# A hybrid decoder layer on one core: gate chunks one head group later, memory K/V beside the last heads, inputs and weights prepared earlier

## The chip, the cores and the metric

The kernel runs on one core of a Trainium2 chip. The metric is the device time of one execution in microseconds (us). A profiled execution gives a trace of every instruction on the core's engines: TensorE (PE, its weight loads apart as PEld), VectorE (DVE), ScalarE (ACT), GpSimd (POOL) and SyncE (SP, which issues DMAs here). "L437" means line 437 of the kernel.

## What is computed

One layer of a decoder for 512 tokens of width 2048, all in float32:

```python
xn = rmsnorm(h, g_mix)
q_a, ..., c_q, c_kv, k_r, gate_a, gate_b = split(xn @ w_in)   # one combined projection
o_a = nsa_attention(...)          # 16 heads: compressed blocks, and window/selected keys
o_b = mla_attention(c_q, c_kv, k_r, ...)                      # 16 heads, low-rank q and k/v
h += (sigmoid(gate_a) * (o_a @ w_o_nsa) + sigmoid(gate_b) * (o_b @ w_o_mla)) @ w_out
h += memory_cross_attention(rmsnorm(h), rmsnorm(mem))         # 4 heads, 256 memory tokens
h += square(relu(rmsnorm(h) @ w_ff1)) @ w_ff2
return rmsnorm(h, g_final)
```

## The kernel before

**Precision.** Each float32 operand is split into a high and a low part (`split`: ACT casts a copy, L444, DVE subtracts, L445), and each product is three matmuls of the parts (`mm`, L437 to L439; in the later stages L1725 to L1727). So TensorE needs ACT and DVE to prepare everything that it reads.

**Chunks.** Up to the attention's end, the kernel goes through `chunk`s: four PSUM banks of 128 tokens by up to 512 columns, 16 steps of k (4 in `mla_q`, 2 in `mla_kv`), 12 matmuls a step. Weights come through one stream `W` (three raw units, three split ones; the loads are on SP's queue, L272). `gate(c)` is one such chunk: columns of the first gate, tanh on ACT (L1151), written to DRAM (`d_g`).

**Side work.** The attention heads are generators in a queue (`Side`). After each group of matmuls a chunk calls `side.run(rate / 4)`, and each whole step that has come together queues a few instructions of a head: scores, softmax, transposes, values. A head item is 11 steps, a group of four heads 44. A group whose heads aren't ready spends its steps for nothing. Beside this runs `side.post`, the work behind a chunk: for `mla_q` four ropes on POOL (L521 to L524), then four transposes of heads (L537); for `mla_kv` the four transposes. At a chunk's last k, `end_post` queues all that is left of it.

**Order of `mla`.** `gate(0)`, `mla_q(0)`, `gate(1)`, `mla_kv(0)`. Then for three groups: the heads of the group before become side work, `mla_q(q + 1)`, a gate chunk (`gate(2)`, `gate(3)`; in the third group `mem_k` instead), `mla_kv(q + 1)`. `mem_load` brings the memory rows (loads L1279 and L1283; split L447/L448, squares on ACT and POOL); it is started between `gate(3)` and `mla_kv(2)`, and takes steps at the k of `mla_kv(2)` and `mla_q(3)`. `mem_v` stands last. The rates are in `T`: `rf` for the first group, `rm` for the others, `rk`, `rv` for the memory chunks, `rg` for the gates.

**`mix` and its three stages.** `Gates` (the second gate), `Mixed` (the two output projections, gated) and `Out` (`w_out`) multiply with seven block products in place of eight: 14 passes each, a pass of four units, a unit a 128 by 1024 block of weights and 12 matmuls. A unit's block may be a sum of two or three blocks of weights: the first is loaded by SP (L1513), the others are added by an accumulating load from POOL's queue (L1520) into the same buffer, after the sum before has been split. `prep(i)` casts the units up to i + 1 (`high`, L1525 on ACT), splits those up to i (`low`, L1530 on DVE) and asks for loads up to i + 2 + `LOADS`; it is called with the current unit + `AHEAD`, which is 3. `stat` and `stat_low` (L1607, L1612) prepare the activations of the next pass. `use` takes a pass's banks.

`Gates.x_in` loads a block of the input (L1929, on SP) and multiplies it by the gains, eight products on POOL (L1932). `mix` loads two of the four blocks, calls `loads(4)`, ends the stream, loads the other two, and then prepares the first units (`ahead`), with two side steps behind each. In the first seven passes of `Gates.run` the rest of the heads is side work at rate `rg`.

In `Mixed.use`, when a block is complete, DVE multiplies it by the gate (L2055, 128 by 1024) and, for the second projection, adds it to the first (L2060), at once for both halves.

Buffers come from 40 slots of 128 by 1024, handed out in the order in which they came free, and five pairs, whose areas are lent once the attention is done (`attended`).

Of the kernel before, what the change touches and what calls it, by code (L numbers as in the profile page):

```python
# [28 lines left out]
AHEAD, LOADS = 3, 3  # L29
ZEROS = 9  # L30
T = dict(pace=0.75, r0=4.0, r1=4.4, rm=2.6, rf=2.5, rk=0.8, rv=1.8, rg=1.4, rs=2)
# [365 lines left out]
class Layer:  # L397
# [747 lines left out]
    def gate(self, c, rate):  # L1145

        nc = self.nc

        def evac(tt, ps):
            g = self.Rv(tt, 512)  # L1150
            nc.scalar.activation(g, ps, AF.Tanh, scale=self.rxh[:, tt:tt + 1])  # L1151
            nc.scalar.dma_start(self.d_g[0, tt, :, 512 * c:512 * c + 512], g)

        self.chunk("ga", c, 512, evac, rate)
# [56 lines left out]
    def mla(self, rate):  # L1211

        self.gate(0, T["rf"])
        qs = self.mla_q(0, T["rf"])
        self.gate(1, T["rf"])
        ks, vs = self.mla_kv(0, T["rf"])
        ml = iter(())

        def load(n):
            return lambda k: [next(ml, None) for _ in range(n)]  # L1220

        for q in range(3):
            self.side.add(self.mla_attend(q, qs, ks, vs))
            qs = self.mla_q(q + 1, rate, load(2))
            if q < 2:
                self.gate(2 + q, rate)
            if q == 1:
                self.put(*self.X)
                ml = self.mem_load()
            if q == 2:  # L1230
                drain(ml)
                self.mem_k(T["rk"])
            ks, vs = self.mla_kv(q + 1, rate, load(4))
        self.side.add(self.mla_attend(3, qs, ks, vs))
        self.side.add(self.flush())
        self.mem_v(T["rv"])


    def mix(self):

        self.put(*self.R)
        g, m = Gates(self), Mixed(self)
        self.lp = []
        self.put(*self.cpairs)
        self.lend_pairs([self.pairs.get() for _ in self.cpairs])
        for a in ((0, 0), (1, 0)):
            g.x_in(*a)
        g.loads(4)
        self.side.end_post()
        self.W.end()  # L1250
        for a in ((1, 1), (0, 1)):
            g.x_in(*a)
        for i in range(4):
            g.ahead(i)
            for _ in range(T["rs"]):
                self.side.step()
        g.run(T["rg"], m)
        return m.run()
# [13 lines left out]
    def mem_load(self):  # L1272
        nc = self.nc
        self.MX = []
        self.mslots = [self.slots.get() for _ in range(8)]
        st, sl = self.halves(6)
        self.macc, self.macc_slot = st[4][:, :256], sl[2]
        for j in range(3):
            nc.sync.dma_start(st[j], self.a["memT"][j])  # L1279
        for j in range(8):  # L1280
            b = st[j % 4]
            if j + 3 < 8:
                nc.sync.dma_start(st[(j + 3) % 4], self.a["memT"][j + 3])  # L1283
            for e in range(2):
                k = 2 * j + e
                x, s = b[:, e * 256:e * 256 + 256], self.mslots[j][:, 512 * e:512 * e + 512]
                h = HL(s[:, :256], s[:, 256:])
                self.split(h, x, self.gains[:, G_MEM + k:G_MEM + k + 1])
                self.MX.append(h)
                self.sumsq(x, k, st[5][:, e * 256:e * 256 + 256], self.macc)  # L1290
                yield
        self.put(*sl[:2])

    def mem_k(self, rate):
# [15 lines left out]
        for h in range(4):  # L1310
            ps = self.ft("mk", h, self.MX, rate, n=256, on_k=on1 if h == 1 else None)
            if h:
                evac(h - 1, last)
            last = ps
        evac(3, last)

    def mem_v(self, rate):
# [3 lines left out]
        for u in range(8):  # L1321
            w = self.W.get(("mv", u, 0))
# [129 lines left out]
class Mlp:  # L1452
# [17 lines left out]
    TAG, TAG1 = "f2", "f1"  # L1470
    LAST = (5, 0, 1, 2, 3, 4, 6)
# [165 lines left out]
    def run(self, out):  # L1637
# [9 lines left out]
        for p in range(last):  # L1647
# [10 lines left out]
            for j in range(4):  # L1658
                i = 4 * p + j
                self.copies()  # L1660
                self.prep(i + AHEAD)
# [248 lines left out]
class Gates(Mlp):  # L1910
# [3 lines left out]
    TAG1 = "gs"  # L1914

# [42 lines left out]
    def run(self, rate, m):  # L1958
# [3 lines left out]
        for p in range(last + 1):  # L1962
            n = p % 7
            if p == 1:
                k.lend_pairs([k.pairs.get()])
# [9 lines left out]
            for j in range(4):  # L1975
                if k.late is None and k.prev is None and len(k.lp) < N_PAIRS:
                    k.attended()
                if p < last or j < 2:
                    self.prep(4 * p + j + AHEAD)
# [11 lines left out]
class Mixed(Mlp):  # L1991
# [3 lines left out]
    TAG = "wo"  # L1995

    def __init__(self, k):
        self.begin(k)
        self.A, self.R, self.g = {}, {}, {}

# [26 lines left out]
    def use(self, p, ps):  # L2027
# [22 lines left out]
        for t in range(2):  # L2050
            r = c, 2 * a + t, b
            g = self.g.pop(r[1:])
            if n < 6:
                x = R.pop(r) if c else R[r]
                v.scalar_tensor_tensor(g if c else x, g, 1.0, x, op0=OP.add, op1=OP.mult)  # L2055
                if c:
                    k.put(x)
            if c:
                x = R[0, 2 * a + t, b]
                v.tensor_add(x, x, g)  # L2060
            k.put(g)
# [14 lines left out]
    def run(self):  # L2076
# [4 lines left out]
        for p in range(last + 1):  # L2081
# [10 lines left out]
            for j in range(4):  # L2092
                if p < last or j < 2:
                    self.prep(4 * p + j + AHEAD)
# [4 lines left out]
                if p == last:  # L2099
                    out.ahead(j)  # L2100
                self.part(p, j, ps, range(2))
# [8 lines left out]
class Out(Mlp):  # L2110
# [7 lines left out]
    TAG = "w2"  # L2118
    COPIED = ((), (), (8, 9, 10), (11, 12, 13))
# [58 lines left out]
    def run(self):  # L2178
# [4 lines left out]
        for p in range(last + 1):  # L2183
# [9 lines left out]
            for j in range(4):  # L2193
                self.prep(4 * p + j + AHEAD)
                if j == 0:
                    self.blocks(p + 1)
                if p < last and j < 2:
                    (self.stat_low if j else self.stat)(p + 1, 0)
                if p < 3 and j % 2:
# [85 lines left out]
```

## Time and profile before

| | us |
|---|---|
| median of 3 runs (2881.62 to 2883.32) | 2883.11 |
| the profiled execution, whole | 2878.02 |
| its span, first to last instruction | 2876.2 |
| end of `gate(1)` (last tanh L1151) | 669 |
| end of `gate(2)` | 747 |
| end of `gate(3)` | 826 |
| evacuation of `mla_kv(3)` (L1189) | 898 to 901 |
| evacuation of `mem_v` (L1331), start of `mix` | 937 |
| first block matmul of `Gates` (L1725) | 950 |
| first evacuation of `Mixed` (L2039) | 1170 |

The times of the lower rows count from the span's start. A group's busy time is the sum over its instructions; a wait is the idle time of an engine in front of an instruction, with the instruction or the DMA that ended it. A window's row gives its length, then the busy time of each engine with the number of instructions, then the granted clock of TensorE (1.00 is full), the busy share of the DMA engines and GB/s. A row of the view in order of time gives start, duration, engine, line, operation, tiles, shape and count, and in brackets the wait before it.

### The profile page before, as it was taken

To read this page: it belongs to the slowest core of one execution; us is meant where nothing else is said; L and a number is where in the kernel's file an instruction comes from. 1 tells how busy PE (TensorE), PEld (TensorE's weight loads), DVE (VectorE), ACT (ScalarE), POOL (GpSimd) and SP (SyncE) were. 2 spreads that over 40 slices of the span, in tenths; PEclk is the share of its full clock that TensorE was granted. 3 is DMA by queue.
4 is the path that set the end of the run, shared out by engine and by line. 5 is a ranking of instruction groups with operands and counts; after the bars stand their busy time and mean duration, and the time that the engine had idled before them with its cause. 6 is when DMAs were issued, how large, how long until landed. Compare 5 with 4: busy or idle time off the path is not lost.

```text
span 2876.2 us, 37039 instructions
## 1 busy us (share of the span) xinstructions
PE 2785.0 (97%) x13428; PEld 2331.8 (81%) x13428; DVE 2036.1 (71%) x3215; ACT 1581.9 (55%) x2650; POOL 484.8 (17%) x708
## 2 busy tenths in 40 slices
PE   9999999999989599999999999999999999999998
PEld 8888889888869477777878888888888888888887
DVE  6446767654567576678776787776776788888888
ACT  5435556644556466543465676666666544444445
POOL 4130110011120511111100111111111111111111
PEclk9999999999999799999999999999999999999999
DMA  5231112222233678998742788888899998899986
GB/s 181 86 98 62 63 58 63 74 84 95 92 109 99 180 185 229 263 235 240 185 110 74 177 219 223 200 203 207 217 228 221 248 226 221 221 221 225 245 230 154
DMA packets 158888, 485.29 MB, mean 169 GB/s; under 512 B 16112, under 2 KB 40816, under 8 KB 158704
## 3 DMA queue, kind: packets, MB, share of 16 engines
q0 software_dynamic: 50688, 184.57, 34.1%
q1 hardware_dynamic: 83264, 268.20, 27.0%
q10 hardware_dynamic: 24752, 30.15, 3.0%
q8 instruction: 105, 1.72, 0.2%
q14 instruction: 79, 0.65, 0.1%
HBM read 447.21 MB, written 35.65 MB: 168 GB/s over the span
## 4 chain that ended last, share of the span: by engine, by line
PE 75%; issue 8%; DMA 6%; DVE 5%; ACT 3%; POOL 3%; ACTq 0%; POOLq 0%; SPq 0%; DVEq 0%
PE mm L1726 8%; PE mm L1727 8%; PE mm L437 8%; PE mm L1725 8%; PE mm L439 8%; PE mm L438 8%; PE st L1725 5%; PE st L1727 5%; PE st L1726 5%; DMA s<-wts 3%; DMA d<-wts 2%; PE st L674 2%; DVE s L1530 1%; PE st L438 1%; PE st L439 1%
## 5 line engine op out<-in xcount | busy, mean ns | idle before, releaser
L1725 PE MATMUL mm<-s,s 128*128 128x512 f32 x1440 | 567.2, 394 | 2.6 <-ACT s L1607 2.1
L1726 PE MATMUL mm<-s,s 128*128 128x512 f32 x1440 | 563.5, 391 | 6.4 <-DVE s L1530 6.3
L1727 PE MATMUL mm<-s,s 128*128 128x512 f32 x1440 | 563.5, 391 | 1.8 <-DVE s L1612 0.9
L1525 ACT CAST s<-d 128x1024 fp32r<-128x1024 f32 x276 | 285.9, 1049 | 302.3 <-DMA d<-wts 276.2
L1530 DVE TENSOR_TENSOR s<-d,s 128x1024 fp32r<-128x1024 f32 x276 | 334.5, 1220 | 120.6 <-ACT s L1525 119.7
L437 PE MATMUL mm<-s,s 128*128 128x512 f32 (+5 forms) x1012 | 399.9, 395 | 0.5 <-ACT s L1161 0.5
L439 PE MATMUL mm<-s,s 128*128 128x512 f32 (+5 forms) x1012 | 381.9, 377 | 0.4 <-DVE s L448 0.4
L438 PE MATMUL mm<-s,s 128*128 128x512 f32 (+5 forms) x1012 | 381.1, 377 | 0.0
L1530 DVE TENSOR_TENSOR s<-s,s 128x1024 fp32r<-128x1024 f32 x248 | 299.3, 1220 | 99.3 <-ACT s L1525 92.4
L1525 ACT CAST s<-s 128x1024 fp32r<-128x1024 f32 x248 | 255.5, 1050 | 189.2 <-DMA s<-wts 163.9
L1726 PE MATMUL st<-s,s 128*128 128x512 f32 x868 | 339.7, 391 | 7.8 <-DVE s L1530 7.8
L1725 PE MATMUL st<-s,s 128*128 128x512 f32 x868 | 341.7, 394 | 0.7 <-ACT s L1607 0.7
L1727 PE MATMUL st<-s,s 128*128 128x512 f32 x868 | 339.7, 391 | 0.9 <-DVE s L1612 0.6
L1726 PEld LDWEIGHTS mm<-s,s 128*128 128x128 f32 x1440 | 271.7, 189 | 63.8 <-DVE s L1530 8.9
L1727 PEld LDWEIGHTS mm<-s,s 128*128 128x128 f32 x1440 | 271.3, 188 | 60.8 <-DVE s L1612 2.7
L1725 PEld LDWEIGHTS mm<-s,s 128*128 128x128 f32 x1440 | 271.5, 189 | 58.6 <-ACT s L1607 2.6
L1520 POOL DMA_DIRECT2D d<-wts x178 | 156.4, 880 | 884.7 <-DVE s L1530 695.9
L445 DVE TENSOR_TENSOR s<-s,s 128x512 fp32r<-128x512 f32 (+4 forms) x301 | 208.2, 701 | 120.8 <-ACT s L444 119.4
L444 ACT CAST s<-s 128x512 fp32r<-128x512 f32 (+4 forms) x301 | 177.1, 602 | 76.3 <-PE mm L439 34.5
L439 PEld LDWEIGHTS mm<-s,s 128*128 128x128 f32 x1012 | 190.0, 188 | 34.0 <-DVE s L448 1.6
L444 ACT CAST s<-st 128x512 fp32r<-128x512 f32 (+4 forms) x249 | 112.7, 460 | 178.5 <-PE st L674 109.7
L437 PEld LDWEIGHTS mm<-s,s 128*128 128x128 f32 x1012 | 191.0, 189 | 22.2 <-ACT s L1161 0.8
(380 smaller groups left out, 4766.1 us busy)
## 6 DMA issues: line engine op xcount, KB each, us to landing
s<-wts SPq DMA_DIRECT2D x240, 512.0 KB, 4.1
d<-wts POOLq DMA_DIRECT2D x178, 512.0 KB, 8.7
s<-wts POOLq DMA_DIRECT2D x115, 512.0 KB, 9.4
d<-wts SPq DMA_DIRECT2D x98, 512.0 KB, 8.4
PP<-wts POOLq DMA_DIRECT2D x59, 512.0 KB, 8.9
PP<-wts SPq DMA_DIRECT2D x33, 512.0 KB, 7.7
d_u<-s ACTq DMA_DIRECT2D x64, 256.0 KB, 5.6
s<-d_u SPq DMA_DIRECT2D x16, 512.0 KB, 11.8
```

The lines of the kernel that those rows point to most:

```text
L437: t.matmul(ps, a.hr, b.hr, start=first, stop=False)
L438: t.matmul(ps, a.hr, b.lr, start=False, stop=False)
L439: t.matmul(ps, a.lr, b.hr, start=False, stop=last)
L444: nc.scalar.copy(o.hr, src)
L445: nc.vector.tensor_sub(o.lr, src, o.hi)
L674: nc.tensor.transpose(ps[:rows, i * 128:i * 128 + 128], p, self.ident)
L1520: self.nc.gpsimd.dma_start(t, src, accum_op=OP.add)
L1525: self.nc.scalar.copy(t.hr, self.raw[i])
L1530: self.nc.vector.tensor_sub(t.lr, r, t.hi)
L1725: m(ps, a.hr, b.hr, start=first, stop=False, skip_group_check=True)
L1726: m(ps, a.hr, b.lr, start=False, stop=False, skip_group_check=True)
L1727: m(ps, a.lr, b.hr, start=False, stop=last, skip_group_check=True)
```

## The change

Five things are changed. The gate chunks move by one head group: `gate(1)` to `gate(3)` run beside the heads, `gate(0)` alone stands in front, at a higher rate (`rf` 4.4 for 2.5). `mem_load` is stepped inside `gate(3)` and `mla_kv(3)`, with the slots of `X` given back one by one. `mem_k` and `mem_v` move behind `mla_kv(3)` into `mix`, and three of the four `x_in`, and the first loads of the gates' weights, are issued inside them; the side steps behind `ahead` go. The gating of `Mixed` goes into a queue, `late`, of which one entry is issued a unit (`settle`). `AHEAD` becomes `FORE` per stage: 4 in `Gates` and `Out`, 5 in `Mixed`, 3 in the MLP as before.

```diff
-AHEAD, LOADS = 3, 3
+LOADS = 3
-T = dict(pace=0.75, r0=4.0, r1=4.4, rm=2.6, rf=2.5, rk=0.8, rv=1.8, rg=1.4, rs=2)
+T = dict(pace=0.75, r0=4.0, r1=4.4, rm=2.6, rf=4.4, rk=0.8, rv=1.8, rg=1.4)
...
     def mla(self, rate):
 
+        def fed(k):
+            if k:
+                self.put(self.X[k - 1])
+            if k == 3:
+                self.ml = self.mem_load()
+            if k == 3 or k > 5:
+                next(self.ml)
+
         self.gate(0, T["rf"])
         qs = self.mla_q(0, T["rf"])
-        self.gate(1, T["rf"])
         ks, vs = self.mla_kv(0, T["rf"])
-        ml = iter(())
-
-        def load(n):
-            return lambda k: [next(ml, None) for _ in range(n)]
-
         for q in range(3):
             self.side.add(self.mla_attend(q, qs, ks, vs))
-            qs = self.mla_q(q + 1, rate, load(2))
-            if q < 2:
-                self.gate(2 + q, rate)
-            if q == 1:
-                self.put(*self.X)
-                ml = self.mem_load()
+            qs = self.mla_q(q + 1, rate)
+            self.gate(1 + q, rate, fed if q == 2 else None)
             if q == 2:
-                drain(ml)
-                self.mem_k(T["rk"])
-            ks, vs = self.mla_kv(q + 1, rate, load(4))
+                self.put(self.X[-1])
+            ks, vs = self.mla_kv(q + 1, rate, (lambda k: [next(self.ml) for _ in range(2)]) if q == 2 else None)
         self.side.add(self.mla_attend(3, qs, ks, vs))
         self.side.add(self.flush())
-        self.mem_v(T["rv"])
 
     def mix(self):
 
-        self.put(*self.R)
+        drain(self.ml)
         g, m = Gates(self), Mixed(self)
         self.lp = []
         self.put(*self.cpairs)
         self.lend_pairs([self.pairs.get() for _ in self.cpairs])
-        for a in ((0, 0), (1, 0)):
-            g.x_in(*a)
-        g.loads(4)
+        self.mem_k(T["rk"], g)
+        self.mem_v(T["rv"], g)
         self.side.end_post()
+        self.put(*self.R)
         self.W.end()
-        for a in ((1, 1), (0, 1)):
-            g.x_in(*a)
+        g.x_in(0, 1)
         for i in range(4):
             g.ahead(i)
-            for _ in range(T["rs"]):
-                self.side.step()
         g.run(T["rg"], m)
...
     def mem_load(self):
-        self.mslots = [self.slots.get() for _ in range(8)]
+        self.mslots = []
...
             nc.sync.dma_start(st[j], self.a["memT"][j])
+        yield
         for j in range(8):
+            self.mslots.append(self.slots.get())
...
     def mem_k(self, rate, g):
         for h in range(4):
+            if h < 3:
+                g.x_in(*((0, 0), (1, 0), (1, 1))[h])
...
     def mem_v(self, rate, g):
         for u in range(8):
+            if u > 3:
+                g.loads(u - 3)
...
# Gates.run
-            if p == 1:
-                k.lend_pairs([k.pairs.get()])
...
# Mixed.use
         for t in range(2):
             r = c, 2 * a + t, b
-            g = self.g.pop(r[1:])
             if n < 6:
-                x = R.pop(r) if c else R[r]
-                v.scalar_tensor_tensor(g if c else x, g, 1.0, x, op0=OP.add, op1=OP.mult)
-                if c:
-                    k.put(x)
+                self.late.append(lambda r=r: self.gated(r))
             if c:
-                x = R[0, 2 * a + t, b]
-                v.tensor_add(x, x, g)
-            k.put(g)
+                self.late.append(lambda r=r: self.added(r))
+            elif n == 6:
+                k.put(self.g.pop(r[1:]))
+
+    def gated(self, r):
+        g, x = self.g[r[1:]], self.R[r]
+        self.nc.vector.scalar_tensor_tensor(g if r[0] else x, g, 1.0, x, op0=OP.add, op1=OP.mult)
+        self.k.put(self.R.pop(r) if r[0] else self.g.pop(r[1:]))
+
+    def added(self, r):
+        g, x = self.g.pop(r[1:]), self.R[0, r[1], r[2]]
+        self.nc.vector.tensor_add(x, x, g)
+        self.k.put(g)
+
+    def settle(self):
+        if self.late:
+            self.late.popleft()()
...
# Mixed.run, in front of each unit's matmuls; Out.run: the same in its first two passes
+                self.settle()
...
# the four stages' run
-                    self.prep(4 * p + j + AHEAD)
+                    self.prep(4 * p + j + self.FORE)
```

More of the change, by code (lines that the diff above doesn't have):

```diff
@@ L1143, in proj_m, with gate @@
             self.side.post = post(c)
-    def gate(self, c, rate):
+    def gate(self, c, rate, on_k=None):
         nc = self.nc
@@ L1152, in evac @@
             nc.scalar.dma_start(self.d_g[0, tt, :, 512 * c:512 * c + 512], g)
-        self.chunk("ga", c, 512, evac, rate)
+        self.chunk("ga", c, 512, evac, rate, on_k=on_k)
     def mla_q(self, q, rate, on_k=None):
@@ L1292, in mem_load, with mem_k @@
         self.put(*sl[:2])
-    def mem_k(self, rate):
+    def mem_k(self, rate, g):
         nc = self.nc
@@ L1315, in mem_k, with mem_v @@
         evac(3, last)
-    def mem_v(self, rate):
+    def mem_v(self, rate, g):
         nc = self.nc
@@ L1470 @@
     TAG, TAG1 = "f2", "f1"
+    FORE = 3
     LAST = (5, 0, 1, 2, 3, 4, 6)
@@ L1660, in run @@
                 self.copies()
-                self.prep(i + AHEAD)
+                self.prep(i + self.FORE)
                 if j == 0:
@@ L1914 @@
     TAG1 = "gs"
+    FORE = 4
     def __init__(self, k):
@@ L1995 @@
     TAG = "wo"
+    FORE = 5
     def __init__(self, k):
@@ L1999, in __init__ @@
         self.A, self.R, self.g = {}, {}, {}
+        self.late = deque()
     def in_last(self, p):
@@ L2093, in run @@
                 if p < last or j < 2:
-                    self.prep(4 * p + j + AHEAD)
+                    self.prep(4 * p + j + self.FORE)
                 if j == 0:
@@ L2118 @@
     TAG = "w2"
+    FORE = 4
     COPIED = ((), (), (8, 9, 10), (11, 12, 13))
@@ L2193, in run @@
             for j in range(4):
-                self.prep(4 * p + j + AHEAD)
+                self.prep(4 * p + j + self.FORE)
                 if j == 0:
@@ L2198, in run @@
                     (self.stat_low if j else self.stat)(p + 1, 0)
+                if p < 2:
+                    self.mixed.settle()
                 if p < 3 and j % 2:
```

## The prediction

> **What bounds the kernel now.** The profile's page comes first: its header, the engines' shares and the granted clock in 40 slices.
>
> ```profile
> span 2876.2 us, 37039 instructions
> PE 2785.0 (97%) x13428; PEld 2331.8 (81%) x13428; DVE 2036.1 (71%) x3215; ACT 1581.9 (55%) x2650; POOL 484.8 (17%) x708
> PEclk9999999999999799999999999999999999999999
> ```
>
> TensorE is busy for 97% of the span. The change removes no matmul, so only two things can shorten the time: the waits of TensorE, 2876.2 − 2785.0 = 91.2 us, and the time at a lower clock. The second view is the windows, cut at the waits; the first number behind each window is its length, the second TensorE's busy time, and three numbers from the end stands the granted clock.
>
> ```profile
> 600.00:830.00 230.00, 229.34 (x1197) 195.07 (x1194) 126.75 (x330) 114.00 (x271) 24.93 (x56) 1.00 0.28 92
> 830.00:841.13 11.13, 0.11 (x1) 0.00 (x0) 7.19 (x14) 8.23 (x23) 5.71 (x8) 0.69 0.54 183
> 841.13:844.48 3.35, 3.35 (x10) 3.35 (x11) 2.66 (x6) 3.35 (x10) 0.93 (x4) 0.50 0.01 2
> 844.48:938.73 94.25, 89.59 (x578) 80.68 (x577) 70.72 (x179) 61.74 (x146) 17.44 (x31) 1.00 0.36 114
> 938.73:946.95 8.22, 0.01 (x1) 0.00 (x1) 1.24 (x4) 4.11 (x7) 8.22 (x10) 0.58 1.02 392
> 946.95:953.71 6.76, 6.76 (x20) 5.41 (x21) 6.63 (x14) 5.18 (x11) 6.76 (x5) 0.50 0.88 282
> 963.00:980.69 17.69, 0.02 (x1) 0.00 (x0) 1.03 (x3) 3.57 (x5) 12.23 (x14) 0.53 0.44 79
> 980.69:984.43 3.74, 3.74 (x11) 3.05 (x12) 3.70 (x8) 2.08 (x7) 0.87 (x1) 0.50 1.18 203
> 984.43:1022.00 37.57, 32.89 (x162) 25.74 (x161) 30.98 (x56) 22.22 (x41) 3.47 (x4) 1.00 0.57 137
> 1022.00:1135.50 113.50, 113.37 (x500) 93.25 (x498) 76.33 (x71) 68.31 (x77) 20.08 (x23) 1.00 0.91 230
> 1135.50:1213.00 77.50, 69.84 (x286) 55.23 (x286) 50.33 (x47) 46.14 (x55) 13.97 (x16) 0.96 0.91 238
> 1213.00:1295.00 82.00, 78.60 (x339) 64.47 (x338) 64.59 (x64) 41.04 (x48) 13.94 (x16) 0.98 0.94 249
> 1295.00:1445.00 150.00, 144.71 (x660) 117.72 (x659) 122.88 (x131) 68.28 (x93) 23.54 (x27) 1.00 0.80 207
> 1445.00:1483.00 38.00, 31.91 (x132) 25.24 (x131) 26.07 (x30) 21.87 (x35) 4.39 (x5) 0.96 0.74 190
> 1483.00:2876.00 1393.00, 1379.66 (x6302) 1141.52 (x6300) 1071.72 (x1202) 793.67 (x995) 223.45 (x256) 1.00 0.82 204
> ```
>
> Three things are to be seen. From 600 to 830, and from 1483 on, TensorE hardly waits, so nothing there can be won. All large waits lie between 830 and 1483, in the stages that the change rearranges. And after a long wait the matmuls run at half the clock for 3.35, 6.76 and 3.74 us, which costs half of each: 1.7, 3.4 and 1.9 us.
>
> **The change, part by part.** All terms are worked out against the profiled execution (2878.0 us, span 2876.2) and then taken off the median, 2883.1; the 5 us between them stay as they are.
>
> *Memory rows loaded inside the last gate chunk: −12.7.* The view of the instructions in order of time shows the wait in front of 841.
>
> ```profile
> 827.71 2.34 SPq L1279 DMA_DIRECT2D s<-memT  x3
> 832.75 0.51 ACT L447 ACTIVATE s<-s,gains 128x256 fp32r<-128x256 f32 x1 [5.63 <-DMA s<-memT]
> ```
>
> `mem_load` issues its first loads between `gate(3)` and `mla_kv(2)`, and ACT stands 5.63 us for them with the evacuation of `mla_kv(2)` queued behind; TensorE waits for its banks, 11.13 − 0.11 = 11.0 us, plus 1.7 of clock. Afterwards the loads go out at k = 3 of `gate(3)` and the first split comes at k = 6. Three steps of k are 36 matmuls, 8.3 us at the spacing 0.23 that the next rows show, without the side work between them; the loads were landed 832.75 − 827.71 = 5.0 us after their issue. The ten splits moved there (0.5 us of ACT each for the split, as much for the square) lie beside a chunk in which ACT is busy half the time (114.00 of 230). Without that cover the 12.7 would stay.
>
> *`mla_q(0)` straight into `mla_kv(0)`: +6.5.* In front of `mla_kv`, `end_post` queues the ropes on POOL and the heads' transposes on TensorE after only one k of `mla_kv`; the other 12 matmuls of `mla_kv(0)` stand behind the transposes, and its evacuation behind those. Today `gate(1)` lies between.
>
> ```profile
> 609.15 0.33 PE L439 MATMUL mm<-s,d 128*128 128x384 f32 x1
> 609.32 0.39 PE L437 MATMUL mm<-s,s 128*128 128x512 f32 x1
> 609.55 0.40 PE L438 MATMUL mm<-s,s 128*128 128x512 f32 x1
> 616.40 0.46 POOL L524 TENSOR_TENSOR s<-rp,rp 128x128 f32<-128x128 f32 x1
> ```
>
> The last matmul of `mla_q(0)` issues at 609.15 and the last rope on POOL ends at 616.86, so the transposes are free 616.86 − 609.32 = 7.5 us after it. The cover is one k, 12 matmuls at the spacing 0.23, 2.7 us; NSA's leftover side steps (74 at `gate(0)`) are used up, since 60 · 1.1 + 12 · 1.1 = 79 are called for. That leaves 4.8 us of wait, plus half of 3.4 us at the low clock, 1.7. Bounds: 0, if leftover steps fill it, to 4.8 + 3.4. I take 6.5, the rows of the same ropes. The other three head groups keep the order of 600 to 830, with 0.66 us of wait in all.
>
> *Memory K/V beside the last heads: −2.7.* The window 844.48 to 938.73 holds 94.25 − 89.59 = 4.7 us of wait, mostly at the two hand-overs to `mem_k` and `mix`.
>
> ```profile
> 862.83 0.31 PE L537 MATMUL st<-cst,s 128*96 128x128 f32 x1 [1.94 <-POOL s L524]
> ```
>
> This one is the ropes of `mla_q(3)` beside the short matmuls of `mem_k`; afterwards `gate(3)` covers them. New is `mla_kv(3)` straight in front of `mem_k`: six memory splits stand around its evacuation on ACT. Between 0 and 5 us; I take 2, near this row. The three inputs of the gates that are loaded in `mem_k` put six loads in front of the memory weights on SP and 24 products on POOL:
>
> ```profile
> 932.97 2.04 SPq L1929 DMA_DIRECT2D d<-xT  x4
> ```
>
> That is 3 us of SP, against three units of weights that the stream holds ready, and 24 · 0.98 (15.67 / 16, below) = 23.5 us of POOL, which works 17.44 of the 94.25 us here. Both are hidden; uncovered, the 3 us would be TensorE's.
>
> *Second gate's input early, side work out of the gates: −4.7, −20.9, −4.7.* The views in order of time around `mix`:
>
> ```profile
> 937.07 1.27 ACT L1331 ACTIVATE s<-mm,rm 128x512 f32<-128x512 f32 x2
> 940.46 1.04 ACT L1607 CAST s<-d 128x1024 fp32r<-128x1024 f32 x1 [2.12 <-POOL d L1932]
> 946.82 1.23 DVE L1530 TENSOR_TENSOR s<-d,s 128x1024 fp32r<-128x1024 f32 x1
> 949.44 1.21 DVE L1612 TENSOR_TENSOR s<-d,s 128x1024 fp32r<-128x1024 f32 x1
> 956.05 15.67 POOL L1932 TENSOR_SCALAR s<-s,gains 128x256 f32<-128x256 f32 x16
> 962.58 0.44 PE L674 MATMUL st<-cst,PP 128*128 128x128 f32 x2 [3.34 <-DVE mx L596]
> 977.12 1.04 ACT L1525 CAST s<-d 128x1024 fp32r<-128x1024 f32 x1 [24.00 <-DMA d<-wts]
> ```
>
> Start of the gates: 8.2 us of wait and 3.4 of clock, 11.6. Afterwards three of four inputs are multiplied by the gains during `mem_k`, but the chain behind the last matmul of `mem_v` stays: evacuation 1.27, two casts 2.08, subtraction 1.23, block's low part 1.21, 5.8 in series; the first matmul needs only the casts, so I take 5.2 of wait and 1.7 of clock: 6.9, −4.7.
>
> The pass behind it: POOL works 15.67 us through 16 gain products, and only then issues the accumulating loads that stand behind them; ACT stands 24.00 us for the first. Waits 3.34 + 17.7, clock 1.9: 22.9. Afterwards only the eight products of the last input are left in front, with their input loadable while `mem_v` runs. Then the first part of unit 5's buffer is split at 7.0 (5.8 + 1.2), the accumulating load lands 8.7 later (the median of page part 6, below), and cast, subtraction and low part make it ready at 7.0 + 8.7 + 1.0 + 1.2 + 1.2 = 19.1, against the pass's end on TensorE at 6.9 + 48 · 0.227 = 17.8. I take 2 of wait (0 to 10): −20.9.
>
> ```profile
> d<-wts POOLq DMA_DIRECT2D x178, 512.0 KB, 8.7
> ```
>
> 984 to 1022: 37.57 − 32.89 = 4.7 us, all at side steps inside the gates. The rates give the three middle groups (60 + 12 + 4) · 0.65 = 49.4 steps each, `mem_k` 64 · 0.4 = 25.6 and `mem_v` 16 · 1.8 = 28.8, in all 203; the heads need 4 · 44 + 6 and about 18 spent on heads that aren't there yet, 200. So they end with `mem_v`, the gates have no side work, and the 113.50 window shows such passes without a wait, at a DMA share of 0.91. The side work itself moves and costs the same.
>
> *Gating queued, weights prepared further ahead: −18.5.* From 1135.5 to 1483 the four windows hold 7.7 + 3.4 + 5.3 + 6.1 = 22.5 us of wait, and 3.1 + 1.6 + 1.5 = 6.2 of clock (length times what the clock lacks).
>
> ```profile
> 1134.30 0.72 ACT L1952 ACTIVATE s<-s,rxh 128x512 f32<-128x512 f32 x1 [4.77 <-DMA d<-d_nsa]
> 1209.58 0.70 PE L1726 MATMUL st<-s,s 128*128 128x512 f32 x1 [1.96 <-DVE s L1530]
> 1209.58:1213.00 3.42, 3.42 (x8) 2.75 (x9) 3.42 (x4) 3.42 (x5) 0.60 (x1) 0.52 1.04 226
> 1288.67 1.22 DVE L2060 TENSOR_TENSOR s<-s,s 128x1024 f32<-128x1024 f32 x1
> ```
>
> Two waits (1209.58, and the 3.4 of the window to 1295) come when L2055 and L2060 stand on DVE in a row in front of the split L1530: 2.0 + 3.4 + 3.1 of clock = 8.5. One such product of 1.22 us a step fits in the 2.7 us of a step: gone. Of the other 20.2 some are late loads (4.77), which an earlier request helps and a full queue does not; between 0 and all, I take half, 10.
>
> The row at 1209.58 also bears on the price of a wait: 1.96 us idle, and the next 3.42 us at 0.52 of the clock. [...]
>
> **Sum:** −12.7 + 6.5 − 2.7 − 4.7 − 20.9 − 4.7 − 18.5 = −57.7; 2883.1 − 57.7 = **2825.4 us** (profiled: 2820).
>
> **Rivals.** *The passes stay as they are:* more units ahead ask no less of a queue at 0.91 and 0.94, and ACT holds at the landing as before. For it: the 4.77 row. Against it: the 113.50 window, as full and without a wait. 2825.4 + 18.5 = 2844.
>
> *The gates' start stays late:* the last input's load goes out only when the weight stream gives its buffers back; 8.7 to land and eight products, half of 15.67, put the accumulating loads 11 us late, with 1.7 of clock: 2838. Against it: buffers freed by earlier heads are taken first.
>
> *Slower:* in Gates, Mixed and Out the casts of one or two further units now stand on ACT in front of the current pass's evacuation.
>
> ```profile
> ACT s L1525 <- DMA d<-wts: 276.2, 109, 24.0
> ```
>
> A cast waits 276.2 / 109 = 2.5 us at the mean for its load. Should 2 us of that reach TensorE in each of the 42 passes, it costs 84 us: 2909. It decides from (57.7 + 5.8) / 42 = 1.5 us a pass. Against it: a bank is needed again only two passes, 22 us, later.
>
> **How the numbers follow.** A measurement tells 0.2%, 5.8 us, from no change. Forecast within about 11 us: 0.50. Passes unchanged: 0.22. Late start: 0.10. Better than 2814 (nothing left of the passes' waits, no new wait at the hand-overs): 0.08. Same: 0.04. Slower: 0.06. Faster is 0.50 + 0.22 + 0.10 + 0.08 = 0.90. The range runs from 2809 (all 28.7 of the passes, both waits of 2 and a third of the 6.5 gone) to 2852 (none of the passes' 18.5, and 8 more at the gates' start).
>
> **What would show it.** No wait on L1189 after the last gate chunk; a new wait of 4 to 5 us on POOL's L524 at `mla_kv(0)`; no 24 us wait of ACT; gates without score matmuls; no L1530 wait behind gating in Mixed. I am wrong if the stream of weights starves in `gate(3)` or `mem_k`, where input loads now stand in front of it on SP.

## The result, and the profile after

The changed kernel takes 2847.5 us (median of 4 runs, 2842.1 to 2851.2) beside 2882.4 for the kernel before: a ratio of 0.988, 95% interval 0.9861 to 0.9899. That is 34.9 us faster, where 57.7 were forecast; 2847.5 lies inside the range of 2809 to 2852, near its upper end.

The execution that was profiled took 2851.24 us, 3.7 above the median, and the profiled one of before, 2878.02, lies 4.3 below its kernel's median of these runs. So the two traces differ by 26.8 us, and the 8.1 us up to 34.9 are scatter of the executions. The accounts below are of the traces.

From the page of the changed kernel, the header and the engines' shares:

```profile
span 2849.4 us, 37079 instructions
PE 2791.6 (98%) x13428; PEld 2337.2 (82%) x13428; DVE 2033.9 (71%) x3215; ACT 1582.1 (56%) x2650; POOL 479.8 (17%) x708
```

TensorE's waits fell from 91.2 us to 2849.4 − 2791.6 = 57.8, which is 33.4 less. Its busy time rose by 6.6 with the same 13428 matmuls: more time at the low clock (0.94 from 560 to 640 and 0.95 from 985 to 1135, where the kernel before had 1.00). −33.4 + 6.6 = −26.8, the whole difference. How much low clock an execution gets is partly chance: a second trace of the changed kernel (`r_after` below) has a span of 2848.1 us and 2787.1 of busy time, 2.1 above the kernel before, with 61.0 us of waits.

The windows, with the columns as before (length, busy time of PE, PEld, DVE, ACT and POOL, granted clock, DMA share, GB/s). First one row of the kernel before, for a stage that the prediction did not quote:

```profile
560.00:640.00 80.00, 79.52 (x418) 67.77 (x417) 45.00 (x136) 39.37 (x103) 7.69 (x16) 1.00 0.26 87
```

And the changed kernel's:

```profile
560.00:640.00 80.00, 73.16 (x367) 61.38 (x367) 44.02 (x149) 40.49 (x108) 7.51 (x20) 0.94 0.19 63
640.00:845.00 205.00, 205.00 (x1088) 176.07 (x1087) 120.20 (x306) 109.54 (x260) 26.58 (x58) 1.00 0.29 96
845.00:945.00 100.00, 97.11 (x601) 86.24 (x599) 76.16 (x196) 66.68 (x164) 37.38 (x42) 1.00 0.53 179
945.00:962.00 17.00, 11.25 (x38) 8.16 (x37) 8.84 (x9) 9.24 (x12) 10.80 (x12) 0.80 0.43 100
962.00:985.00 23.00, 22.00 (x96) 17.54 (x95) 16.67 (x15) 11.25 (x13) 3.52 (x5) 1.00 0.93 214
985.00:1135.00 150.00, 140.10 (x584) 112.57 (x583) 98.13 (x90) 88.04 (x99) 24.37 (x28) 0.95 0.84 216
1135.00:1483.00 348.00, 334.17 (x1482) 272.41 (x1481) 266.07 (x279) 180.14 (x245) 52.23 (x60) 0.98 0.79 205
1483.00:2849.00 1366.00, 1353.59 (x6162) 1120.13 (x6160) 1052.03 (x1178) 777.14 (x963) 222.86 (x256) 1.00 0.84 208
```

Two stages are as hoped: the 11 us hole before 841 is gone (640 to 845 has no wait at all), and so is the 17.7 us hole at 963 (962 to 985 has 1.0). Two are worse than before: 560 to 640, where nothing was priced but the hand-over to `mla_kv(0)`, and 985 to 1135, which was to run without a wait and has 9.9 us of waits at a mean clock of 0.95. The waits of TensorE by line from 945 to 1500 (us in total, times, longest) show how their nature changed. Before:

```profile
PE st L437 <- DVE s L445: 18.0, 2, 17.7
PE st L674 <- DVE s L445: 8.2, 1, 8.2
PE st L1726 <- DVE s L1530: 7.8, 3, 3.4
PE mm L1726 <- DVE s L1530: 6.3, 5, 3.4
```

and after:

```profile
PE mm L1725 <- ACT s L1607: 8.2, 3, 5.0
PE mm L1725 <- ACT s L1525: 4.9, 1, 4.9
PE mm L1727 <- DVE s L1612: 3.4, 7, 0.7
...
PE mm L1725 <- ACT s L2167: 3.0, 2, 2.1
...
PE st L1725 <- DVE d L2048: 1.8, 1, 1.8
...
PE mm L1726 <- DVE s L1530: 0.5, 1, 0.5
```

Before, TensorE waited for weights (L1530, their low part). Now weights are ready once the stage runs (0.5 us; the 4.9 for L1525 are its first matmul), and it waits for its activations: L1607 and L1612 in `Gates` and `Mixed`, L2167 in `Out`. They are made on the same ACT and DVE that prepare the weights. The view in order of time, ACT alone, shows why, around 1027:

```profile
1010.78 0.33 ACTq L1955 DMA_DIRECT2D d_g<-s  x1
...
1022.36 1.05 ACT L1525 CAST s<-s 128x1024 fp32r<-128x1024 f32 x1 [6.36 <-DMA d_g<-s]
1023.31 0.72 ACT L1953 ACTIVATE s<-s,rxh 128x512 f32<-128x512 f32 x1
...
1026.56 1.04 ACT L1607 CAST s<-d 128x1024 fp32r<-128x1024 f32 x1
```

and the next row of TensorE, a matmul that reads that last cast:

```profile
1027.65 0.50 PE L1725 MATMUL mm<-s,s 128*128 128x512 f32 x1 [2.28 <-ACT s L1607]
```

At `FORE` 4, the last `prep` of a pass casts the first unit of the pass after the next. ACT stands 6.36 us in front of that cast, until 1022.36, and not for the unit's weights. In the trace the cast waits for three transfers: its accumulating load, issued at 997.68 and landed at 1009.2, and the two writes of the gate block that has just been evacuated, of which the second, issued at 1010.78, landed at 1022.3. The DMA view of these two issues, with the time to landing at the end:

```profile
s<-wts POOLq DMA_DIRECT2D x1, 512.0 KB, 11.5
...
d_g<-s ACTq DMA_DIRECT2D x1, 256.0 KB, 11.5
```

`Gates.use` gives the block's slot back as soon as its writes are issued, and every cast of a unit takes two slots; so a cast further ahead is handed a slot that a write still reads. (The views name no slots; that it is the same one follows from the program and from what the cast waits for.) The evacuation (L1953) and the activations (L1607), which could be done at once, stand behind; the activations are needed by the same matmul as the held unit. When ACT is free, DVE and TensorE follow at once: the split of the held unit at 1023.44, 0.03 us behind its cast, and the matmul at 1027.65, 0.05 us behind the cast of its activations. Of the 9.9 us of waits from 985 to 1135, 2.28 come here; the largest, 4.99 us, has another cause, shown further down.

### The profile page after: what moved, and what is told of

It reads as the page before. It is cut to its first block, busy times and chain, and to the rows that moved or that the text cites. A ratio compares the mean times of both kernels' runs of the same rounds, so it can differ in the third digit from the quotient of the medians.

```text
span 2849.4 us, 37079 instructions
## 1 busy us (share of the span) xinstructions
PE 2791.6 (98%) x13428; PEld 2337.2 (82%) x13428; DVE 2033.9 (71%) x3215; ACT 1582.1 (56%) x2650; POOL 479.8 (17%) x708
## 4 chain that ended last, share of the span: by engine, by line
PE 74%; issue 9%; DMA 7%; DVE 4%; ACT 3%; POOL 2%; ACTq 0%; SPq 0%; POOLq 0%; DVEq 0%
PE mm L1727 8%; PE mm L1725 8%; PE mm L1726 8%; PE mm L437 8%; PE mm L439 7%; PE mm L438 7%; PE st L1727 5%; PE st L1725 5%; PE st L1726 5%; DMA s<-wts 4%; PE st L674 2%; DMA d<-wts 2%; DVE s L1530 1%; PE st L438 1%; PE st L439 1%
## 5 line engine op out<-in xcount | busy, mean ns | idle before, releaser
L1725 PE MATMUL mm<-s,s 128*128 128x512 f32 x1440 | 570.5, 396 | 16.1 <-ACT s L1607 8.2
L1525 ACT CAST s<-d 128x1024 fp32r<-128x1024 f32 x272 | 282.0, 1049 | 262.3 <-DMA d<-wts 236.0
L1530 DVE TENSOR_TENSOR s<-d,s 128x1024 fp32r<-128x1024 f32 x272 | 329.8, 1220 | 107.6 <-ACT s L1525 105.9
L1530 DVE TENSOR_TENSOR s<-s,s 128x1024 fp32r<-128x1024 f32 x248 | 299.9, 1220 | 138.1 <-ACT s L1525 137.9
L1525 ACT CAST s<-s 128x1024 fp32r<-128x1024 f32 x248 | 255.7, 1049 | 207.6 <-DMA s<-wts 180.3
L1520 POOL DMA_DIRECT2D d<-wts x170 | 148.4, 873 | 880.9 <-DVE s L1530 684.0
```

The lines of the kernel that those rows point to most:

```text
L1520: self.nc.gpsimd.dma_start(t, src, accum_op=OP.add)
L1525: self.nc.scalar.copy(t.hr, self.raw[i])
L1530: self.nc.vector.tensor_sub(t.lr, r, t.hi)
L1725: m(ps, a.hr, b.hr, start=first, stop=False, skip_group_check=True)
```

## The experiments

Two theories are set against each other. The step on record says that units prepared further ahead, and the gating queue, take waits away. Theory A says that a cast of a further unit stands on ACT in front of what the next pass needs, and so costs. Medians are compared with the changed kernel's second set of runs:

> The changed kernel again, as the measure for the three runs beside it. Every theory: 2842 to 2851 us, as in its first four runs; between the second pass of the gates and the end of the third block stage TensorE waits some 23 us, nearly all of it for L1607, L1612, L2167 and L2172 (activations of the next pass) or for banks, and almost none for L1530 (weights).

Measured: 2851.2 us (2849.0 to 2853.5), 0.9892 [0.9877, 0.9907]. The waits are as expected in kind, 0.5 us for L1530, and 25.5 us from 985 to 1483. The two medians of one kernel, 2847.5 and 2851.2, lie 3.7 us apart, so differences below 4 us are not read here. The kernel before took 2881.6 to 2882.5 us beside each set of runs. Against the first median, 2847.5, every gain below would be 3.7 us smaller.

### One unit less ahead

`FORE` = 3 in all three stages:

```diff
# Gates
-    FORE = 4
+    FORE = 3
# Mixed
-    FORE = 5
+    FORE = 3
# Out
-    FORE = 4
+    FORE = 3
```

> The changed kernel with the weights prepared three units ahead in all stages, as before. My prediction's step (further ahead takes waits away): slower than the changed kernel by up to 10 us, with waits for L1530 back in Mixed and Out. Rival A (the casts of further units stand on ACT, waiting for their loads, in front of the evacuation and of the next pass's activation): faster by 5 to 12 us, the waits for L1607 and L2167 shrink. Rival B (only the loads' landing and the wait of a gate write for an earlier load set the waits): within 3 us.

Measured: 2839.6 us (2837.2 to 2842.1), 0.9851 [0.9836, 0.9867]: 11.7 us faster. The waits of TensorE from 945 to 1500:

```profile
PE mm L1726 <- DVE s L1530: 5.6, 6, 2.6
...
PE mm L1725 <- ACT s L1607: 2.7, 2, 2.5
...
PE st L1726 <- DVE s L1530: 2.0, 1, 2.0
```

The waits for L1607 fall from 8.2 to 2.7 and those for L2167 are gone; the weights' (L1530) come back with 7.6. By the last view ACT reaches the same cast in time:

```profile
1015.69 1.05 ACT L1525 CAST s<-s 128x1024 fp32r<-128x1024 f32 x1 [0.40 <-ACT s L1953]
1016.64 1.05 ACT L1607 CAST s<-d 128x1024 fp32r<-128x1024 f32 x1
```

Here the evacuations (L1953) come first, and the cast waits for no write and no load. The time goes as theory A says, and against the step on record. But `FORE` sets three things at once, how far the casts, the splits and the requests for loads run ahead (`prep`); a kernel that casts as late and asks for its loads as early wasn't tried. In which stage?

```diff
# Gates alone; Mixed keeps 5, Out 4
-    FORE = 4
+    FORE = 3
```

> FORE = 3 in Gates alone; Mixed keeps 5 and Out 4. Theory A (a cast of a further unit stands on ACT in front of the next pass's activations, and costs wherever the accumulating loads are close): about half of what FORE = 3 everywhere brought (11.7 us against the 2851.2 of the changed kernel), from the waits of Gates at 1027, 1064 and 1104 and the time at half clock behind them: 2843 to 2848. If the gain of FORE = 3 everywhere came from Mixed and Out alone (less DMA asked for, no cast in front of use): 2850 to 2853. If all came from Gates: 2838 to 2841.

Measured: 2839.8 us (2837.8 to 2844.4), 0.9855 [0.9842, 0.9869]. All of the gain comes from `Gates`; half was expected. A window of this kernel:

```profile
985.00:1135.00 150.00, 144.50 (x613) 116.36 (x614) 103.13 (x95) 91.39 (x103) 27.06 (x31) 0.98 0.90 230
```

From 985 to 1135 the waits fall from 9.9 to 5.5 us, the clock rises from 0.95 to 0.98, and the DMA share rises from 0.84 to 0.90; that buffers come free sooner when ACT is not held is the likely reason, not shown. Of the 4.4 us, 2.4 are at the largest wait, 4.99 us, which is 2.6 here. In `Mixed` and `Out` 3 and 5 units (or 4) cost the same, 2839.6 and 2839.8 us: waits for L1530 in the one, for L2167 in the other.

### The activations in front of the casts

The other way to the same end, at the `FORE` of the changed kernel; the same swap in the three stages:

```diff
-                if p < last or j < 2:
-                    self.prep(4 * p + j + self.FORE)
                 if p < last:
                     (self.stat_low if j % 2 else self.stat)(p + 1, j // 2)
-                else:
+                if p < last or j < 2:
+                    self.prep(4 * p + j + self.FORE)
+                if p == last:
                     m.ahead(j)
```

> The changed kernel with the activation of the next pass queued in front of the weight casts of each unit in Gates, Mixed and Out, and the weights as far ahead as in the change. Rival A: faster by 5 to 12 us, with the waits for L1607, L1612, L2167 and L2172 mostly gone. Rival B: within 3 us. My prediction's step says nothing against either: it counted no such wait.

Measured: 2845.0 us (2843.5 to 2846.2), 0.987 [0.9853, 0.9885]: 6.3 us faster, in the band of rival A. But the waits that rival A names are not "mostly gone": those for L1607, L1612, L2167 and L2172 are 16.7 us from 945 to 1500, against 17.5 and 19.3 in the two traces of the changed kernel. The hold is still there, since the held cast stands at the end of a pass and the activations at the start of the next; ACT and then TensorE:

```profile
1019.93 1.05 ACT L1525 CAST s<-s 128x1024 fp32r<-128x1024 f32 x1 [6.11 <-DMA d_g<-s]
...
1024.22 0.50 PE L1725 MATMUL mm<-s,s 128*128 128x512 f32 x1 [2.16 <-ACT s L1607]
```

What is shorter is the wait of 4.99 us near 1104 (6.2 in the second trace), which is 1.6 here. So the time went the way of theory A, but not by the wait that it names; why this order is faster is not shown. And with `FORE` = 3 in all stages on top:

> FORE = 3 everywhere, and the next pass's activations issued in front of the casts. Theory A (both edits remove the same wait, of the activations behind a cast on ACT): not the sum of the two gains (11.7 and 6.3) but that of FORE = 3 alone, 2836 to 2841. If they were two independent causes: the sum, 2831 to 2835. If both gains were something else, as a smaller DMA demand: also the sum or less than the larger gain, above 2841.

Measured: 2845.6 us (2842.8 to 2849.6), 0.9874 [0.9861, 0.9888]. That is a miss: not the 2839 of `FORE` = 3 alone, but 6 us more, in the band that was set for "something else". The waits of this kernel from 945 to 1500:

```profile
PE mm L1726 <- DVE s L1530: 12.1, 13, 3.2
PE mm L1725 <- ACT s L1525: 8.1, 4, 4.9
...
PE st L1726 <- DVE s L1530: 3.1, 4, 1.2
```

No wait for L1607 is left, but now the weights are late, for 15.2 us behind L1530 alone. Theory A, "the activations behind a cast", does not carry these two results: at `FORE` = 3 the cast is due in the same pass, and to put the activations in front of it makes the weights late. What the traces do show is narrower: at `FORE` = 4 in `Gates`, a cast that waits for the landing of writes (6.36 us, at 1022.36) holds what stands behind it on ACT, and at 3 it does not (0.40 us, at 1015.69).

### The gating at once, without its queue

```diff
             if n < 6:
-                self.late.append(lambda r=r: self.gated(r))
+                self.gated(r)
             if c:
-                self.late.append(lambda r=r: self.added(r))
+                self.added(r)
```

> The changed kernel with the gating products of Mixed issued at once in place of one a unit. My prediction's step: slower by 5 to 9 us (two waits of 2 to 3.4 us and their time at the lower clock come back behind L2055 and L2060). Rival (five units ahead already cover such a run of products on DVE): within 2 us.

Measured: 2851.5 us (2850.4 to 2853.8), 0.9894 [0.9879, 0.9908]. The queue brings nothing beside five units ahead: TensorE's waits for L1530 stay at 0.5 us without it, as in the changed kernel. The waits behind the products do come back, for another split: from 1205 to 1300 TensorE waits 1.4 and 1.7 us for L1612, each behind four products in a row on DVE. With the queue (second trace) it waits as long there, 1.9 and 2.1 us, for evacuations (L2048, L2046). With `FORE` = 3 and the queue the waits for L1530 are 7.6, with neither (the kernel before) 14.1. Which part took away the rest of the waits in `Mixed` and `Out` wasn't settled: both undone together, with the rest of the change kept, wasn't tried.

### The gates' input as late as before

Two blocks in front of the end of the weight stream, two behind it, none in `mem_k`:

```diff
# mem_k
-            if h < 3:
-                g.x_in(*((0, 0), (1, 0), (1, 1))[h])
# mix
         self.mem_v(T["rv"], g)
+        for a in ((0, 0), (1, 0)):
+            g.x_in(*a)
         self.side.end_post()
         self.put(*self.R)
         self.W.end()
-        g.x_in(0, 1)
+        for a in ((1, 1), (0, 1)):
+            g.x_in(*a)
```

> The changed kernel with the four inputs of the second gate loaded where they were before: two in front of the end of the stream, two behind it (the rest of the change stays, the side steps stay out of the gates). My prediction's step (products on POOL and their loads in front of the accumulating loads made the waits of 8 and 24 us): slower than the changed kernel by 15 to 30 us, with a wait of ACT of 15 us or more for an accumulated load near 970. Rival (the waits at the gates' start came from the heads' side steps in the gates, which are gone either way): within 5 us.

Measured: 2861.3 us (2859.5 to 2862.9), 0.9927 [0.9912, 0.9942]: 10.0 us slower. Its windows:

```profile
962.00:1010.00 48.00, 27.47 (x110) 21.66 (x109) 23.49 (x21) 18.42 (x21) 22.33 (x26) 0.79 0.59 122
1010.00:1135.00 125.00, 122.37 (x533) 99.24 (x532) 88.08 (x83) 79.55 (x90) 21.16 (x25) 1.00 0.91 238
...
970.63:991.11 20.48, 4.84 (x11) 3.35 (x12) 7.08 (x6) 4.09 (x4) 10.50 (x12) 0.50 0.70 128
```

The stall is back in full, with 20.5 us of wait. The low clock lasts 20.48 us, but TensorE is busy for only 4.84 of them, so it costs 2.4: some 23 us in all. The passes behind it, at the same `FORE` = 4, now lose 2.6 us of wait and nothing of clock, against 9.9 and 7.5 from 985 in the changed kernel. So more than half of what the stall costs, 14.8 of some 23 us, is missing again in these passes, and removing it is worth 10 us net, less than the 15 to 30 expected.

It is not that the loads and casts run ahead while TensorE stands. ACT stands for 27.19 us, until 981.48, and the DMA engines stand for about half of the time from 964 to 986, 19 of the 40 digits being 0 (each is the busy share of a fortieth, in tenths):

```profile
DMA  0000157950000000000000009689999999999999
```

Nor are the casts further ahead afterwards: the first cast for the third pass starts 6.1 us before the matmul that needs it, for 5.3 in the changed kernel, and for the sixth 7.4, for 7.6. What these passes lack are the two long holds of ACT in the changed kernel, 6.36 us at 1022 (the cast in its place waits for no write) and 7.10 at 1102 (2.5 here). Why they don't come behind the stall is open.

### The start of the heads

The changed kernel's view in order of time around 566, ACT and then TensorE:

```profile
560.40 1.28 ACT L481 ACT_TABLE_LOAD   x1
...
563.04 1.28 ACT L597 ACT_TABLE_LOAD   x1
...
565.98 0.50 PE L697 MATMUL o<-s,s 128*128 128x512 f32 x1 [1.11 <-ACT s L444]
566.84 0.50 PE L698 MATMUL o<-s,s 128*128 128x512 f32 x1 [0.36 <-DVE s L445]
```

In `gate(0)`, at the new rate 4.4, side work follows so closely that of two table loads on ACT, 1.28 us each, 1.11 and 0.36 us reach TensorE as waits for the casts and splits behind them. The rate down to 3.6:

```diff
-rf=4.4
+rf=3.6
```

> The changed kernel with the rate of the first head group at 3.6 in place of 4.4. Theory (at 4.4 the heads' chain runs out of matmuls to hide behind: 3.5 us of waits between 565 and 620 that my sum didn't hold, and 3.4 us of clock): those waits shrink, faster by 3 to 7 us; the nine side steps left over fall into mla_kv(0) and the next group, which wasted seven. Rival (the wait at 566 comes from ACT's table loads there at any rate): within 2 us.

Measured: 2840.8 us (2838.3 to 2844.1), 0.9857 [0.9842, 0.9871]: 10.4 us faster. The window of this kernel:

```profile
560.00:640.00 80.00, 76.47 (x427) 66.39 (x425) 50.35 (x162) 45.60 (x123) 7.85 (x20) 1.00 0.23 76
```

3.5 us of wait and none of clock, for 6.8 and 4.8 (6.8 and 1.6 in the second trace). The steps that the slower rate leaves over may also fill part of the hand-over at 633. So the waits at the heads' start shrink as the theory says, but the 10.4 us, more than the 3 to 7 expected, are not explained by them: over the whole span the waits are 58.8 us, for 57.8 and 61.0 in the two traces of the changed kernel, and what is smaller is the busy time, 2780.0 for 2791.6 and 2787.1, with the same matmuls: less time at the low clock (0.995 at the mean of the profiled execution, for 0.991 and 0.993). The other edit aims at that hand-over alone:

```diff
         self.gate(0, T["rf"])
-        qs = self.mla_q(0, T["rf"])
         ks, vs = self.mla_kv(0, T["rf"])
+        qs = self.mla_q(0, T["rf"])
```

> The changed kernel with mla_kv(0) in front of mla_q(0), so that the ropes get the three steps of k of mla_q(1) as cover. My prediction's step (7.5 us of ropes against one step of k): the waits of TensorE for L524 and L445 at 630 (4.4 us, and 1.7 us of clock) shrink to 1 or 2, faster by 3 to 5 us. Rival (other side work arrives later in exchange, and the wait turns up at the next group): within 2 us.

Measured: 2844.7 us (2841.6 to 2845.6), 0.9867 [0.9851, 0.9884]: 6.6 us faster, against 3 to 5 expected. The window of this kernel has 0.6 us of wait and full clock, for 3.3 of wait and 1.7 of clock in the changed kernel; that the 6.6 meet the 6.5 that the prediction had put on the hand-over is in part chance:

```profile
625.00:640.00 15.00, 14.41 (x91) 14.01 (x90) 6.40 (x10) 6.71 (x14) 7.33 (x16) 1.00 0.35 109
```

### The blocks of `Mixed` from another queue

The largest wait of the passes, 4.99 us at 1104.94, has its own cause. SP's row and ACT's in the changed kernel:

```profile
1081.03 7.76 SPq L2010 DMA_DIRECT2D d<-d_nsa  x3
...
1102.53 0.33 ACTq L1955 DMA_DIRECT2D d_g<-PP  x1
1102.89 1.04 ACT L1525 CAST s<-s 128x1024 fp32r<-128x1024 f32 x1 [7.10 <-DMA d<-d_nsa]
```

ACT doesn't issue the write of a gate (L1955) until a block of `Mixed`, requested by SP at 1081, has landed some 21 us later, and the activations (L1607, at 1103.84) stand behind it. The write doesn't need the block's data. In the trace both count on one semaphore: the queue's wait for it ends at 1102.47, when the load has landed, and then the write is issued with it. The blocks from POOL's queue instead:

```diff
# Mixed.blocks
-            self.nc.sync.dma_start(...)
+            self.nc.gpsimd.dma_start(...)
```

> The changed kernel with the activation blocks of Mixed loaded from POOL's queue in place of SP's, so that the gate writes on ACT no longer take the semaphore of such a load. Theory (a gate write waits for the earlier load of d_nsa on the same semaphore, 7.1 us of ACT, 5 us of TensorE and 3.4 of clock near 1104): that wait goes, faster by 4 to 9 us. Rival (ACT then waits as long for the weights, or POOL's accumulating loads come later): within 3 us or slower.

Measured: 2858.9 us (2854.6 to 2862.7), 0.9918 [0.9903, 0.9933]: 7.6 us slower. The wait at 1104 goes, but the blocks now stand among the accumulating loads on POOL, and the waits for L1607, by the same view as above, come elsewhere and more often:

```profile
PE mm L1725 <- ACT s L1607: 7.6, 5, 3.4
...
PE st L1725 <- ACT s L1607: 5.2, 2, 3.7
```

### Together

`FORE` = 3 and `rf` = 3.6, both edits as above:

> FORE = 3 everywhere and rf = 3.6. The two act on stages far apart (565 to 640, and 1025 to 1480), so theory A says that the gains add up: 2851.2 - 11.7 - 10.4 = 2829, between 2826 and 2833. If a part of either gain was the clock's chance state or comes back as a later wait on the loads (TensorE reaches Gates at the same distance from its weights, so this should not be): 2834 to 2840.

Measured: 2835.1 us (2831.9 to 2837.2), 0.9836 [0.9822, 0.9849], the best of all and 16.1 us below the changed kernel. 2829 was expected from the sum of the gains, and 2834 to 2840 if a part of either was chance. What is missing, 6 us, is little more than the medians scatter: from the first median, 2847.5, the two gains are 7.9 and 6.7, and their sum gives 2832.9. All four edits:

> FORE = 3, rf = 3.6, mla_kv(0) in front of mla_q(0), and the activations in front of the casts. Theory A: the fourth shares its wait with the first, and the third shares the wait at 633 with the second (of whose gain 2.4 us of wait are left there), so it brings only 2 to 4 us beyond the first two: 2824 to 2830. If all four were independent: 2851.2 - 11.7 - 10.4 - 6.6 - 6.3 = 2816. If the order on ACT bites elsewhere (use behind the activations): 2831 to 2838.

Measured: 2835.4 us (2833.6 to 2838.1), 0.9836 [0.9822, 0.9849], no better. The order of `mla_kv(0)` and `mla_q(0)` brings the first matmul of the gates forward from 944.68, in the kernel with two edits, to 941.85; the activations in front cost it again, as they do with `FORE` = 3 above: the waits for L1530 are 14.4 us here and 15.2 there. The time lies in the band set for an order on ACT that bites elsewhere.

## Why the prediction was right, and where it was wrong

By its own steps, forecast and measured in the two traces (waits as length less busy time, clock as length times what it lacks; the clock has two digits, so a long row is good to 1 or 2 us):

| step | forecast | measured |
|---|---|---|
| memory rows inside the last gate chunk | −12.7 | −12.7: no wait from 640 to 845 |
| `mla_q(0)` into `mla_kv(0)` | +6.5 | +5.0: 3.3 of waits at 631 to 637, 1.7 of clock |
| the rate of `gate(0)` | not priced | +6.1: the rest of 560 to 640 (6.8 + 4.8 − 5.0), less 0.5 before |
| memory K/V | −2.7 | −1.8: 2.9 us left from 845 to 945 |
| start of the gates | −4.7 | −2.4: 5.75 + 3.4 = 9.2 for 11.6 |
| the pass behind it | −20.9 | −21.9: 1.0 left |
| gate passes without side work | −4.7 | +12.6: 9.9 + 7.5 for 4.8 from 985 to 1135 |
| gating queued, weights further ahead | −18.5 | −7.9: 13.8 + 7.0 for 28.7 |
| sum | −57.7 | −23.0 |

The traces differ by 26.8; 0.9 of the remaining 3.8 are fewer waits behind 1483, the rest is spread thinly and wasn't followed.

**Right:** the direction, and the three mechanisms that carried it: the memory rows, the second gate's input, and the bare hand-over to `mla_kv(0)`, where the wait is for the ropes as forecast, but smaller: 2.8 us for L524 and 0.5 for a split, where 4.8 were worked out.

**Luck:** that 2847.5 lies inside the range. The centre was missed by 22 us, twice the 11 that had the chance of 0.50. The upper end stood for none of the passes' 18.5 and 8 more at the gates' start; in the traces 7.9 of the 18.5 came and the gates' start went as forecast within 2.3, and the loss came from gate passes that the sum had counted as a gain.

**Wrong, the largest: "the gates have no side work, and the 113.50 window shows such passes without a wait".** The gates do run without side work. But that window was measured some 40 us behind a stall of 22.9 us, and with three units ahead, not four. Neither was a property of "such passes". With the stall back, the passes are smooth even at four units (the kernel with late input), though not by a lead of the loads; with three units in `Gates` 5.5 us of wait are left for 9.9. What the sum did not hold are the two holds of ACT, by a cast that waits for the landing of writes (6.36 us) and by a gate write that waits for a load (7.10 us).

**Wrong: "gating queued, weights prepared further ahead, −18.5".** The 8.5 for the queue: taking it out changed the time by +0.3 us; the waits behind the products, 3.1 us, come back for L1612, and others of the same size go. The 10 for more units ahead: in `Mixed` and `Out` three units are as fast, and in `Gates` the fourth costs 11.4 us (2851.2 against 2839.8). The rival "the passes stay as they are", 2844, came nearer to the time, though the passes did not stay: the waits for weights went, and waits for activations took their place. The rival "slower" had that mechanism, casts of further units on ACT in front of the pass's own work, with the wrong cause, a load where the trace shows the landing of two writes, at 1022.3, and the wrong victim: it named the evacuation, whose bank is not needed for two passes, where the activations issued behind it are needed at once. Its price of 1.5 us a pass was reached in few passes. The row with 4.77 us at 1134.30, which the prediction took for a late load, is a gate write's hold of the kind at 1102: the write at 1133.93 waits until a block of `d_nsa` has landed on the semaphore that both use.

**Wrong, an edit without a price:** the rate `rf` was used to count side steps, but its own effect, ACT and DVE that don't keep up inside `gate(0)`, was put at nothing without naming a cover. It cost some 6 us in the trace; how the 10.4 us of the slower rate divide is open, as said above.

**Clock.** The sum had the low clock only behind the waits that it kept. The new waits are short, but from 985 to 1135 the trace has 3.41, 3.41 and 6.83 us at half clock beside them (from 1028.90, 1066.45 and 1104.00), half of which is 1.7, 1.7 and 3.4 us; by the row's 0.95, 7.5 of the 17.4 us lost there are clock.

## What to carry to other kernels

Preparing further ahead can put what must wait in front of what could be done: here ACT stood 6.36 us in front of one cast, with evacuations and activations behind it. Before counting the gain, ask what else that engine must issue between, and what can hold the extra item: not its load alone (landed at 1009.2 here), but the buffer that it is to write (the writes that, by the program, still read it landed at 1022.3). A stretch that runs smoothly behind a stall is no evidence for what it does once the stall is gone: here more than half of what the stall cost, 14.8 of some 23 us, came back as smaller waits and low clock. And a time that comes out as a theory says does not yet show its mechanism: the trace must lose the wait that the theory names. A rate at which side work is called for is a cost of its own, here 10.4 us between 4.4 and 3.6, and wants a price like any moved step.

## What the runs showed of the hardware

The price of a short wait was not fixed: 0 in one trace and 1.7 us in another. TensorE's wait of 2.35 us for the evacuation of `mla_kv(3)` is the same in two kernels. Windows of the changed kernel, the wait and what follows:

```profile
877.93:880.28 2.35, 0.00 (x1) 0.01 (x1) 2.35 (x5) 2.35 (x8) 2.24 (x5) 1.00 0.01 4
880.28:883.70 3.42, 3.42 (x27) 3.33 (x28) 3.03 (x6) 3.42 (x10) 1.26 (x3) 1.00 0.06 11
```

and of the one with `FORE` = 3:

```profile
874.62:876.97 2.35, 0.01 (x1) 0.00 (x0) 2.35 (x5) 2.35 (x8) 2.24 (x5) 1.00 0.00 0
876.97:878.46 1.49, 1.49 (x12) 1.49 (x13) 1.14 (x3) 1.49 (x5) 0.41 (x2) 1.00 0.00 0
878.46:881.87 3.41, 3.41 (x16) 3.19 (x15) 3.36 (x6) 3.41 (x11) 1.64 (x2) 0.50 0.38 97
```

The same wait costs nothing in the one and 1.7 us in the other (half of 3.41), where the low clock begins 1.49 us behind the wait and lasts 3.41. Even waits of 1.11 and 0.36 us, at 566 in the changed kernel, were followed by twice that time at half clock:

```profile
568.10:574.93 6.83, 6.83 (x21) 5.50 (x20) 2.40 (x11) 1.39 (x5) 0.00 (x0) 0.50 0.14 53
```

In the second trace of that kernel the same two waits, 1.08 and 0.36 us, were followed by none: the clock is 1.00 from 560 to 600.

The stretches at half clock last 3.41 and 6.83 us in these windows. What decides whether a wait is followed by one, and when, is not shown.

A write that ACT issues waited 7.1 us, at 1102, for another queue's load that it doesn't read. Both count on one semaphore in the trace, and moving that load to POOL's queue took the wait away: there the cast behind the write, at 1093.96, stood 0.40 us, for the evacuation. A cast of weights that had landed at 1009.2 waited until 1022.36 for the landing of writes to DRAM that ACT itself had issued at 1009.65 and 1010.78.
